# Softmax sums of two head groups folded into the head norm's epsilon, in a two-layer hybrid trunk

## The chip, the cores and the metric

One core of one Trainium2 chip runs the whole program. The metric is the device time of one execution in microseconds (us). Three executions of the kernel before gave 1511.83, 1502.17 and 1504.89 us, a median of 1504.89. The execution that the profiler recorded took 1500.35 us, of which 1498.6 us lie between its first and last instruction (its span).

The engines are TensorE (PE in the profile, with its weight loads as PEld), VectorE (DVE), ScalarE (ACT) and GpSimd (POOL). SyncE (SP) issues most DMAs. Each takes its own instructions strictly in the order in which they were laid down.

## The reference, cut to what matters

Two layers on 512 positions of width 1024. A layer has a mixer of four head groups (A sparse attention, B retention, C gated linear attention, D differential attention), each four heads of 64, and then a squared-ReLU MLP. What the change touches is the end of groups A and D:

```python
def head_norm(y, g, center, dtype):
    ...
    yf = yf * lax.rsqrt(jnp.mean(yf * yf, axis=-1, keepdims=True) + EPS)     # EPS = 1e-6
    yf = yf * g
# group A: one map for each head
    p = jax.nn.softmax(s, axis=-1)
    out = einsum(p, v_sel)
# group D: two maps for each head, a learned lambda
    p = jax.nn.softmax(s, axis=-1)
    w = p[:, :, 0] - lam * p[:, :, 1]
    out = einsum(w, v)
```

A head's output goes straight into `head_norm`. If the softmax is left without its division by the sum m of its row, the output y is m times larger, and the norm gives the same result when eps is replaced by eps times m squared.

## The kernel before, in words

Activations lie as 128 features by 512 positions; weights and activations are split into a high and a low part (`whi`, `wlo`, by ACT and by DVE or POOL), and a projection takes three matmuls for each pair (lines 268 to 270, tiles `ptm`, `ptc`, `po`, `pf`, `p`).

`mixers(l, ...)` (from line 571) emits one layer's mixer. Keys and queries of the indexer come first, then group A's top-k selection on DVE: 48 pairs of MAX8 and MATCH_REPLACE8 (lines 810, 811) for each layer. Then group C in chunks, then D, A and B. The order of D, A and B and of the remaining projections is the token string `PLAN['seq']`: `D00` is head pair 0, block 0 of group D, `8.1` the second row block of projection 8, and so on. Blocks are 128 queries; block b looks at W = 128(b+1) keys.

For a block, `softmax_scores` (line 598) subtracts the row's maximum on DVE (line 602, with the scale and the mask), takes Exp on ACT with the row's sum as a second result (line 604), and takes the sum's reciprocal on DVE (line 608). `d_block` (line 1009) does this for the two maps of each of two heads. It then scales the second map by its reciprocal and by minus lambda (line 1029) and adds the first, scaled by its own (line 1030). `a_block` (line 1042) scales its one map (line 1052), on DVE in six of eight blocks and on ACT in two (`PLAN['xa']`). `pv_block` (line 612) transposes the maps on PE (line 618), copies them out on ACT (line 620) and multiplies by the values (line 623) into one PSUM tile, `yd` or `ya`, of a pool with a single buffer (`yp`). After block 3 `headnorm` (line 580) squares that tile on ACT (`hq`, line 583), sums over the 64 features of each head by a matmul with a block matrix of ones (`hs`, line 585), takes Ln and Exp (lines 587, 588) and multiplies on DVE (line 595), which frees the PSUM tile.

The modulation vectors are matrix-vector products done on DVE (`gemv`, line 277): one DMA of 512 KB into one of two buffers (`gw`) and one reduction of 1024 elements (line 281). In layer 0, 24 of them (three parts of eight columns) are put behind the tokens of projections 8 and 9 and at the output projection. The list `fence` holds an instruction behind which a product emitted later must stand on DVE:

```python
i = gemv(l, part, j, wp.tile([P, DM], F32, name=f"gw{l}_{part}_{j}", tag="graw", bufs=PLAN["gb"]))
for x in fence:
    after(x, i)
```

`fence` is set in three places: at the start of layer 0 to the scaled input `hr` (line 1206), at the end of a pre-norm (line 525), and in `a_block` to the scaling of the last map (line 1054). `after` orders two instructions of the same engine and adds no semaphore.

What is emitted is not yet the order on the engines. A planner walks the program with its own cost estimates and gives each engine, whenever it is free in that estimate, the ready instruction that was emitted first. The resulting order is fixed for the run.

Of the kernel before, what the change touches and what calls it, by code (L numbers as in the profile page):

```python
# [10 lines left out]
F32 = mybir.dt.float32  # L11
# [3 lines left out]
AF = mybir.ActivationFunctionType  # L15
ALU = mybir.AluOpType
# [5 lines left out]
PLAN = {'ah': {},  # L22
 'ap': 'dddd',
 'ar': 'dddd',
 'blo': 'dppd',
 'br': [0, 0, 0, 1],
 'bst': 2,
 'ce': 's',
 'cp': 1,
 'cq': 'a',  # L30
# [59 lines left out]
P = 128  # L90
L = 2
DM = 1024
T = 512
KT = 8
NB = 4
HT = 256
HD = 64
EPS = 1e-6
# [99 lines left out]
def tile_trunk(ctx: ExitStack, tc: tile.TileContext, a, out, dbg=None):  # L198
    nc = tc.nc
    pe, act, dve, pool, sp = nc.tensor, nc.scalar, nc.vector, nc.gpsimd, nc.sync  # L200
# [28 lines left out]
    msk = cp.tile([P, T], F32, name="msk")  # L229
# [8 lines left out]
    eps = cp.tile([P, 1], F32, name="eps")  # L238
    dve.memset(eps, EPS)
    zero = cp.tile([P, 1], F32, name="zero")  # L240
# [5 lines left out]
    nt = ctx.enter_context(tc.tile_pool(name="nt", bufs=2))  # L246
# [28 lines left out]
    fence = []  # L275
# [56 lines left out]
    for i in range(KT):  # L332
        q = nt.tile([P, T], F32, name=f"first_sq{i}", tag="rs" if i % 2 == 0 else "sq", bufs=RS if i % 2 == 0 else 2)
# [8 lines left out]
        e = PLAN["fs"][i // 2:i // 2 + 1]  # L342
# [15 lines left out]
    def rstd(ps, name, n=HT):  # L358
        r = nt.tile([P, n], F32, name="r" + name, tag="nm_r", bufs=1)
        act.activation(r, ps, AF.Ln, bias=eps, scale=1.0 / DM)  # L360
        m = nt.tile([P, n], F32, name="m" + name, tag="rs", bufs=RS)
        dve.tensor_scalar(m, ps, 1.0 / DM, EPS, ALU.mult, ALU.add)
        e = act.activation(r, r, AF.Exp, scale=-0.5)
        t = nt.tile([P, n], F32, name="t" + name, tag="sq")
        dve.tensor_tensor(t, r, r, ALU.mult)
        dve.scalar_tensor_tensor(t, t, -0.5, m, ALU.mult, ALU.mult)
        done[:] = [dve.scalar_tensor_tensor(r, t, 1.5, r, ALU.add, ALU.mult), e]
        return r
# [68 lines left out]
    r1 = rstd(ss1, "first", T)  # L437
# [132 lines left out]
    E = {"p": pool, "d": dve}  # L570

    def mixers(l, h, ch):
# [3 lines left out]
        s0 = st0.enter_context(tc.tile_pool(name=f"s0{l}", bufs=1, side="right", reuse_waits="tile"))  # L576
        stk = ExitStack()
        mx = stk.enter_context(tc.tile_pool(name=f"mx{l}", bufs=1, reuse_waits="tile"))

        def headnorm(i, src):  # L580

            q = nt.tile([P, T], F32, name=f"hq{l}_{i}", tag="sq")
            act.activation(q, src, AF.Square)
            p2 = pj.tile([P, T], F32, name=f"hs{l}_{i}", tag="pj")
            pe.matmul(p2, blk, q, start=True, stop=True)
            r = nt.tile([P, T], F32, name=f"hr{l}_{i}", tag="nm_r", bufs=1)
            act.activation(r, p2, AF.Ln, bias=eps, scale=1.0 / HD)
            act.activation(r, r, AF.Exp, scale=-0.5)
            g = hg[:, l, i:i + 1]
            if 2 <= i < 6:  # L590
                v = nt.tile([P, T], F32, name=f"hv{l}_{i}", tag="rs", bufs=RS)
                dve.tensor_tensor(v, src, r, ALU.mult)
                dve.scalar_tensor_tensor(Y[i], v, g, Y[i], ALU.mult, ALU.mult)
            else:
                dve.scalar_tensor_tensor(Y[i], src, g, r, ALU.mult, ALU.mult)

        NORM = ALU.divide if PLAN['div'] else ALU.mult

        def softmax_scores(ps, mask, W, scale, name):
            s = nt.tile([P, T], F32, name="s" + name, tag="rs", bufs=RS)[:, :W]  # L600
            mn = mx.tile([P, 1], F32, name="mn" + name, tag="mn", bufs=4)
            dve.tensor_tensor_reduce(s, ps, mask, -scale, 3e38, ALU.add, ALU.min, mn)  # L602
            sm = mx.tile([P, 1], F32, name="su" + name, tag="su", bufs=4)
            act.activation(s, s, AF.Exp, bias=mn, scale=-1.0, accum_out=sm)  # L604
            if PLAN["div"]:
                return s, sm
            rc = mx.tile([P, 1], F32, name="rc" + name, tag="rc", bufs=4)
            dve.reciprocal(rc, sm)
            return s, rc

        def pv_block(ps, b, ss, Vs, name):

# [168 lines left out]
        masks = [msk[:, T - P:]]  # L781
        for b in range(1, NB):
            W = P * (b + 1)
# [3 lines left out]
            for hd in range(8):  # L787
                ps = sc.tile([P, T], F32, name=f"ix{l}_{b}_{hd}", tag="sc")[:, :W]
# [4 lines left out]
                e, t = (pool, acp) if hd in PI else (dve, acc)  # L793
# [36 lines left out]
        sums = s1.tile([P, 9, P], F32R, name=f"sums{l}")  # L830
# [71 lines left out]
        for b in range(NB):  # L902
# [3 lines left out]
            for c in range(4):  # L906
# [3 lines left out]
                for hd in range(4):  # L910
                    r = slice(32 * hd, 32 * hd + 32)
                    e = PLAN["qf"][4 * c + hd]
                    f = {"a": act.copy, "p": pool.tensor_copy, "d": dve.tensor_copy}[e]
                    f(Q[r, :, hd, :], QS4[c // 2][r, 2 * (c % 2):2 * (c % 2) + 2, :])  # L914
                ps = sc.tile([P, 2, 4, 64], F32, name=f"sg{l}_{b}_{c}", tag="sc")
# [20 lines left out]
            for hd in range(4):  # L936
                pr, hh = divmod(hd, 2)
# [5 lines left out]
            if b < NB - 1:  # L943
# [6 lines left out]
                s = s1.tile([P, 256], F32, name=f"S{l}_{b}", tag="S", bufs=2)  # L950
                E[PLAN["ms"]].memset(s, 0.0)
                for hd in range(4):
                    r = slice(32 * hd, 32 * hd + 32)
                    c = slice(64 * hd, 64 * hd + 64)
# [46 lines left out]
        def d_open(pr):  # L1001
            QD.append(s1.tile([P, 4, T], F32R, name=f"QD{l}_{pr}", tag="QD", bufs=2))
            KD.append(s1.tile([P, 4, T], F32R, name=f"KD{l}_{pr}", tag="KD", bufs=2))
            for i in range(2):
                d_parts(pr, i)

        def d_block(pr, b):
            if b == 0:
                if pr == len(QD):
                    d_open(pr)  # L1010
            elif b < NB - 1:
                d_parts(pr, b + 1)
            W = P * (b + 1)
            N = max(W, 256)
            sb = []
            for hh in range(2):
                sr = []
                for c in range(2):
                    m = 2 * hh + c
                    ps = sc.tile([P, T], F32, name=f"sd{l}_{pr}_{m}_{b}", tag="sc")  # L1020
                    pe.matmul(ps[:, :N], QD[pr][:, m, b * P:(b + 1) * P], KD[pr][:, m, :N], start=True, stop=True)  # L1021
                    sr.append(softmax_scores(ps[:, :W], msk[:, T - W:], W, 32 ** -0.5, f"D{l}_{pr}_{m}_{b}"))
                (s0, r0), (s1_, r1) = sr
                z = PLAN["xd"][4 * pr + b]
                if z == "a":
                    dve.tensor_tensor(r1, r1, lamv[l], ALU.mult)
                    act.mul(s1_, s1_, r1)
                else:
                    E[z].tensor_scalar(s1_, s1_, r1, lamv[l], ALU.mult, ALU.mult)
                dve.scalar_tensor_tensor(s0, s0, r0, s1_, NORM, ALU.add)  # L1030
                sb.append(s0)
            top(PLAN['top'][4 * pr + b])
            yield
            if b == 0:
                yh[6 + pr] = yp.tile([P, T], F32, name=f"yd{l}_{pr}", tag="yp")
            pv_block(yh[6 + pr], b, sb, [(lambda j, c=64 * (2 * pr + hh): Vd[:, j, c:c + 64]) for hh in range(2)],
                     f"D{l}_{pr}_{b}")
            if b == NB - 1:
                headnorm(6 + pr, yh[6 + pr])

        def a_block(pr, b):
            if b:
                top(max(0, 16 * b + 1 - taken[0]))
            W = P * (b + 1)
            sb = []
            for hh in range(2):
                nme = f"A{l}_{pr}_{hh}_{b}"
                ps = sc.tile([P, T], F32, name="s" + nme, tag="sc")
                two_pass(ps, QS[:, 2 * pr + hh, b * P:(b + 1) * P], 0, max(W, 256))
                s, rc = softmax_scores(ps[:, :W], masks[b], W, HD ** -0.5, nme)  # L1050
                z = PLAN["xa"][4 * pr + b]
                xx = act.mul(s, s, rc) if z == "a" else E[z].tensor_scalar(s, s, rc, None, ALU.mult)
                if PLAN['fence']:
                    fence[:] = [xx]
                sb.append(s)
            yield
            if b == 0:
                yh[pr] = yp.tile([P, T], F32, name=f"ya{l}_{pr}", tag="yp")
            pv_block(yh[pr], b, sb, [lambda j: Va[:, j, :]] * 2, f"A{l}_{pr}_{b}")
            if b == NB - 1:  # L1060
                headnorm(pr, yh[pr])

        def b_rope(b):
            if b == 0:
# [33 lines left out]
        QD, KD, QB, yh = [], [], [], {}  # L1098
# [8 lines left out]
        for tok in PLAN["seq"].split():  # L1107
            k = tok[0]
# [16 lines left out]
            else:  # L1125
                g, b = tok.split(".")
# [9 lines left out]
    ident = cp.tile([P, P], F32, name="ident")  # L1136
    blk = cp.tile([P, P], F32, name="blk")
# [3 lines left out]
    lamv = [cp.tile([P, 1], F32, name=f"nlam{l}") for l in range(L)]  # L1141
# [228 lines left out]
    h, ch = h_tiles("h10_"), None  # L1370
    for l in range(L):
        h, ch = rest(l, mixers(l, h, ch))
# [26 lines left out]
```

## Time and profile before

| | |
|---|---|
| median of three executions | 1504.89 us (1502.17 to 1511.83) |
| profiled execution | 1500.35 us, span 1498.6 us |
| mean granted TensorE clock | 0.981 |
| PE busy | 1424.6 us, 95% of the span |
| weight loads busy | 1190.9 us, 79% |
| DVE busy | 990.7 us, 66% |
| ACT busy | 742.3 us, 50% |
| POOL busy | 280.5 us, 19% |

Busy shares are means over stages with different limits. The mixers are at about 50 to 330 us (layer 0) and 800 to 1066 us (layer 1) of the span; the rest is output projection and MLP.

### The profile page before, as it was taken

The page shows a single profiled execution, that of the slowest core. Times are in us where ns is not written, and L with a number is a line of the kernel's source. Part 1 is how long each engine was busy: PE and PEld are TensorE (multiplying, and loading weights), DVE is VectorE, ACT ScalarE, POOL GpSimd, SP SyncE. Part 2 cuts the span into 40 slices and gives each one's busy share as a digit, 9 for nine tenths or more (in the row PEclk, how much of TensorE's full clock was granted, in tenths as well). Part 3 has the DMA queues.
Part 4 walks back from the last instruction along what each step waited for, and adds up shares of the span by engine and source line. Part 5 has one row for each costly group of instructions (what it writes and reads, how often), then busy time and mean ns, then how long its engine had stood idle before and what let it go on. Part 6 is the DMA issues. An engine that isn't in the chain of part 4 may idle for free.

```text
span 1498.6 us, 23592 instructions
## 1 busy us (share of the span) xinstructions
PE 1424.6 (95%) x8514; PEld 1190.9 (79%) x8514; DVE 990.7 (66%) x2209; ACT 742.3 (50%) x1655; POOL 280.5 (19%) x268
## 2 busy tenths in 40 slices
PE   7989999999999999999989899999999999999996
PEld 4667878768898878888978769787789888888896
DVE  8798878786796875434477999753678334343435
ACT  4667486656453323324257575855765333242322
POOL 3244321335100000000032443213430000000001
PEclk8999999999999999999999999999999999999999
DMA  9420223466078884333131102211531433333301
GB/s 340 140 68 14 78 71 99 150 205 222 29 245 288 294 268 155 92 99 92 43 113 59 57 15 72 71 43 56 163 104 52 126 93 94 97 97 93 94 20 57
DMA packets 82269, 171.12 MB, mean 114 GB/s; under 512 B 9284, under 2 KB 16102, under 8 KB 81896
## 3 DMA queue, kind: packets, MB, share of 16 engines
q1 hardware_dynamic: 79524, 167.47, 35.7%
q10 hardware_dynamic: 2628, 2.14, 0.4%
q8 instruction: 67, 1.10, 0.3%
q14 instruction: 50, 0.41, 0.1%
HBM read 165.39 MB, written 4.19 MB: 113 GB/s over the span
## 4 chain that ended last, share of the span: by engine, by line
PE 71%; DVE 17%; ACT 4%; DMA 4%; issue 2%; POOL 1%; SPq 0%; DVEq 0%; ACTq 0%; POOLq 0%
PE p L269 7%; PE p L270 7%; PE p L268 7%; PE pf L269 7%; PE pf L270 7%; PE pf L268 7%; PE ptm L268 3%; PE ptm L269 3%; PE ptm L270 3%; DVE ia L797 2%; DVE m L810 2%; DVE ia L811 2%; PE first L1186 1%; DMA gw<-modw 1%; PE firstk L1186 1%
## 5 line engine op out<-in xcount | busy, mean ns | idle before, releaser
L262 ACT CAST whi<-raw 128x512 fp32r<-128x512 f32 x388 | 237.3, 621 | 355.9 <-PE p L269 157.9
L264 DVE TENSOR_TENSOR wlo<-raw,whi 128x512 fp32r<-128x512 f32 x266 | 190.8, 722 | 205.7 <-ACT whi L262 194.1
L264 POOL TENSOR_TENSOR wlo<-raw,whi 128x512 fp32r<-128x512 f32 x122 | 165.1, 1371 | 330.0 <-ACT whi L262 279.7
L461 POOL TENSOR_TENSOR sapost<-sapost,sqpost 128x256 f32<-128x256 f32 x16 | 12.3, 771 | 671.6 <-ACT sqpost L459 671.6
L281 DVE CUSTOM_DVE_ANT_0 gw<-gw,cond 128x1024 f32<-128x1024 f32 x80 | 101.3, 1269 | 40.6 <-DMA gw<-modw 40.2
L810 DVE MAX8 m<-ia 128x8 f32<-128x256 f32 (+2 forms) x96 | 53.1, 556 | 1.3
L811 DVE MATCH_REPLACE8 ia<-m,ia 128x256 f32<-128x256 f32 (+2 forms) x96 | 52.0, 542 | 0.0
L914 ACT COPY QF<-q 32x256 f32<-32x256 f32 x120 | 48.4, 403 | 5.5 <-DVE q L891 2.5
L1288 DVE TENSOR_TENSOR rf<-rf,pf 128x512 f32<-128x512 f32 (+1 forms) x80 | 45.8, 574 | 2.6 <-ACT rf L1287 2.5
L1287 ACT ACTIVATE rf<-pf 128x512 f32<-128x512 f32 (+1 forms) x80 | 40.5, 507 | 5.6 <-PE pf L270 5.6
L923 PE MATMUL sg<-QF,KF 128*64 128x256 f32 x224 | 30.5, 395 | 11.0 <-DVE AC L929 8.2
L602 DVE CUSTOM_DVE_ANT_0 sD<-sd,msk 128x128 f32<-128x128 f32 (+3 forms) x64 | 29.6, 488 | 16.8 <-PE sd L1021 12.0
L604 ACT ACTIVATE sD<-sD,mnD 128x128 f32<-128x128 f32 (+3 forms) x64 | 35.5, 559 | 6.8 <-DVE mnD L602 6.4
L890 POOL TENSOR_TENSOR KF<-F,kc 128x512 f32<-128x512 f32 x16 | 23.9, 1502 | 43.7 <-ACT F L883 42.4
L268 PE MATMUL p<-hd_7h,whi 128*128 128x512 f32 (+1 forms) x80 | 28.6, 358 | 3.1 <-ACT hd_7h L471 3.1
L923 PEld LDWEIGHTS sg<-QF,KF 128*64 128x64 f32 x224 | 14.6, 137 | 21.0 <-issue 13.7
L269 PE MATMUL pf<-h_5l,whi 128*128 128x512 f32 (+1 forms) x80 | 28.0, 350 | 2.8 <-DVE h_5l L515 2.8
L797 DVE SCALAR_TENSOR_TENSOR ia<-rl,wi,ia 128x256 f32<-128x256 f32 (+2 forms) x42 | 29.0, 708 | 2.2 <-ACT rl L791 1.0
L269 PE MATMUL p<-hd_7l,whi 128*128 128x512 f32 (+1 forms) x80 | 28.3, 353 | 0.6 <-DVE hd_7l L472 0.6
L268 PE MATMUL ptm<-whi,h_0h 128*128 128x256 f32 x74 | 25.4, 345 | 3.5 <-ACT h_0h L511 3.5
L467 PE MATMUL sspre<-sapre,ones 128*128 128x256 f32 x48 | 17.3, 474 | 12.0 <-POOL sapre L461 7.1
L268 PE MATMUL p<-hd_0h,whi 128*128 128x512 f32 (+1 forms) x80 | 28.4, 355 | 0.0
(623 smaller groups left out, 5002.2 us busy)
## 6 DMA issues: line engine op xcount, KB each, us to landing
raw<-w SPq DMA_DIRECT2D x256, 256.0 KB, 2.7
gw<-modw SPq DMA_DIRECT2D x80, 512.0 KB, 4.2
raw<-wtm SPq DMA_DIRECT2D x76, 256.0 KB, 2.8
gs<-modw SPq DMA_DIRECT2D x16, 512.0 KB, 6.3
raw<-wo SPq DMA_DIRECT2D x32, 256.0 KB, 2.7
raw<-wtc SPq DMA_DIRECT2D x24, 256.0 KB, 2.8
xin<-xT SPq DMA_DIRECT2D x8, 256.0 KB, 3.5
wq<-wtm SPq DMA_DIRECT2D x8, 256.0 KB, 6.4
```

Source lines behind the costliest of these rows:

```text
L262: act.copy(hi, raw)
L264: (lo_eng or dve).tensor_tensor(lo, raw, bits(hi), ALU.subtract)
L268: pe.matmul(ps, l[0], r[0], start=start, stop=False)
L269: pe.matmul(ps, l[0], r[1], start=False, stop=False)
L270: pe.matmul(ps, l[1], r[0], start=False, stop=stop)
L281: return dve.tensor_tensor_reduce(raw, raw, cond, 1.0, 0.0, ALU.mult, ALU.add, modT[l][:, c:c + 1])
L797: e.scalar_tensor_tensor(t, rl, wi[:, b, hd:hd + 1], t, ALU.mult, ALU.add)
L810: dve.max(m8, acc)
L811: dve.match_replace(acc, m8, acc, MARK)
L914: f(Q[r, :, hd, :], QS4[c // 2][r, 2 * (c % 2):2 * (c % 2) + 2, :])
L923: pe.matmul(ps[t, i], KF[:, lv, t], Q[:, i, :, t], start=True, stop=True)
L1288: dve.tensor_tensor(rl, rl, ps, ALU.mult)
```

## The change

The reciprocals of A's sums, the scaling of A's maps and the setting of `fence` in `a_block` go. The sums of A's map and of D's first map are kept in a tile of 128 by 4 blocks by 2 heads for each head pair. In D the second map is multiplied by minus lambda times m0/m1 and added to the unscaled first map: a reciprocal and one operation on 128 by 1, then one operation on the maps. `headnorm` of the four head pairs of A and D gets the sums: it squares them, scaled by the root of 64 eps and spread over 64 columns (`he`, one ACT operation on 128 by 512), and adds them to the block sum by four matmuls with the identity as moving operand; Ln is then taken with a bias of zero.

```diff
-        def headnorm(i, src):
+        def headnorm(i, src, sums=None):
             q = nt.tile([P, T], F32, name=f"hq{l}_{i}", tag="sq")
             act.activation(q, src, AF.Square)
             p2 = pj.tile([P, T], F32, name=f"hs{l}_{i}", tag="pj")
-            pe.matmul(p2, blk, q, start=True, stop=True)
+            pe.matmul(p2, blk, q, start=True, stop=sums is None)
+            if sums is not None:
+                e = nt.tile([P, NB, 2, HD], F32, name=f"he{l}_{i}", tag="sq")
+                act.activation(e, sums.unsqueeze(3).broadcast_to([P, NB, 2, HD]), AF.Square, scale=(HD * EPS) ** 0.5)
+                for b in range(NB):
+                    pe.matmul(p2[:, P * b:P * b + P], e[:, b].rearrange("p h d -> p (h d)"), ident, start=False, stop=b == NB - 1)
             r = nt.tile([P, T], F32, name=f"hr{l}_{i}", tag="nm_r", bufs=1)
-            act.activation(r, p2, AF.Ln, bias=eps, scale=1.0 / HD)
+            act.activation(r, p2, AF.Ln, bias=eps if sums is None else zero, scale=1.0 / HD)
...
-        def softmax_scores(ps, mask, W, scale, name):
+        def softmax_scores(ps, mask, W, scale, name, sm):
...
-            sm = mx.tile([P, 1], F32, name="su" + name, tag="su", bufs=4)
             act.activation(s, s, AF.Exp, bias=mn, scale=-1.0, accum_out=sm)
-            if PLAN["div"]:
-                return s, sm
-            rc = mx.tile([P, 1], F32, name="rc" + name, tag="rc", bufs=4)
-            dve.reciprocal(rc, sm)
-            return s, rc
+            return s
+
+        heads_sum = {}
+
+        def sum_of(k, pr, b, hh):
+            if (k, pr) not in heads_sum:
+                heads_sum[k, pr] = mx.tile([P, NB, 2], F32, name=f"hsum{l}_{k}{pr}", tag="hsum", bufs=4)
+            return heads_sum[k, pr][:, b, hh:hh + 1]
...
-                (s0, r0), (s1_, r1) = sr
...
-                    E[z].tensor_scalar(s1_, s1_, r1, lamv[l], ALU.mult, ALU.mult)
-                dve.scalar_tensor_tensor(s0, s0, r0, s1_, NORM, ALU.add)
+                (s0, m0), (s1_, m1) = sr
+                rt = mx.tile([P, 1], F32, name=f"rt{l}_{pr}_{hh}_{b}", tag="rc", bufs=4)
+                dve.reciprocal(rt, m1)
+                dve.scalar_tensor_tensor(rt, rt, m0, lamv[l], ALU.mult, ALU.mult)
+                dve.scalar_tensor_tensor(s0, s1_, rt, s0, ALU.mult, ALU.add)
...
-                s, rc = softmax_scores(ps[:, :W], masks[b], W, HD ** -0.5, nme)
-                z = PLAN["xa"][4 * pr + b]
-                xx = act.mul(s, s, rc) if z == "a" else E[z].tensor_scalar(s, s, rc, None, ALU.mult)
-                if PLAN['fence']:
-                    fence[:] = [xx]
-                sb.append(s)
+                sb.append(softmax_scores(ps[:, :W], masks[b], W, HD ** -0.5, nme, sum_of("A", pr, b, hh)))
```

## Rows read from the trace of the kernel before

**Rows 1.** The page: busy us, share of the span, instructions; then the chain's shares.
```profile
PE 1424.6 (95%) x8514; PEld 1190.9 (79%) x8514; DVE 990.7 (66%) x2209; ACT 742.3 (50%) x1655; POOL 280.5 (19%) x268
...
PE 71%; DVE 17%; ACT 4%; DMA 4%; issue 2%; POOL 1%; SPq 0%; DVEq 0%; ACTq 0%; POOLq 0%
```
**Rows 2.** Windows by stage; columns in the first line.
```profile
core 0: us, PE busy (x) PEld busy (x) DVE busy (x) ACT busy (x) POOL busy (x), PEclk, DMA share, GB/s
50.00:182.00 132.00, 119.27 (x792) 95.07 (x791) 118.18 (x310) 87.26 (x220) 58.34 (x57) 0.97 0.21 61
182.00:330.00 148.00, 143.77 (x936) 111.57 (x937) 113.08 (x308) 95.80 (x240) 39.91 (x31) 0.97 0.38 124
922.00:1066.00 144.00, 139.57 (x942) 108.82 (x941) 88.35 (x270) 97.21 (x244) 40.41 (x34) 1.00 0.20 59
```
**Rows 3.** Groups by line, DVE: busy us, mean ns of one, idle before.
```profile
L1030 DVE SCALAR_TENSOR_TENSOR sD<-sD,rcD,sD 128x128 f32<-128x128 f32 (+3 forms) x32 | 20.4, 638 | 0.4
L1029 DVE TENSOR_SCALAR sD<-sD,rcD,nlam 128x128 f32<-128x128 f32 (+3 forms) x32 | 14.7, 459 | 0.9
L1052 DVE TENSOR_SCALAR sA<-sA,rcA 128x128 f32<-128x128 f32 (+3 forms) x24 | 10.9, 455 | 0.5
L608 DVE RECIPROCAL rcD<-suD 128x1 f32<-128x1 f32 x64 | 9.9, 159 | 8.3 <-ACT sD L604 7.6
```
**Rows 4.** Groups by line, ACT: A's scaling, and the head norm's Square.
```profile
L1052 ACT ACTIVATE sA<-sA,rcA 128x256 f32<-128x256 f32 (+1 forms) x8 | 4.2, 555 | 0.2 <-DVE rcA L608 0.2
...
L583 ACT ACTIVATE hq<-yd 128x512 f32<-128x512 f32 x4 | 2.4, 599 | 0.8 <-PE yd L623 0.7
```
**Rows 5.** Timeline of PE at 86 and at 247 us: start, us, instruction.
```profile
86.36 1.15 PE L842 MATMUL z<-wa,caT 17*128 17x128 f32 x8
87.45 0.50 PE L268 MATMUL ptc_t<-h_5h,whi 128*128 128x512 f32 x1
...
247.45 1.02 PE L585 MATMUL hs<-hq,blk 128*128 128x512 f32 x2
247.91 0.68 PE L268 MATMUL ptm<-whi,h_0h 128*128 128x256 f32 x1
```
**Rows 6.** Waits of PE, 182 to 332 us: waiter, releaser, us in total, times, longest.
```profile
PE sd L1021 <- DVE mnD L602: 4.6, 2, 3.6
```
**Rows 7.** The same of layer 1, 915 to 1075 us.
```profile
PE sd L1021 <- DVE mnD L602: 2.1, 2, 1.0
```
**Rows 8.** Timelines of SP and DVE: the products' first DMA, and where products stand.
```profile
42.10 0.33 SPq L279 DMA_DIRECT2D gw<-modw  x1
...
286.97 0.97 DVE L1052 TENSOR_SCALAR sA<-sA,rcA 128x512 f32<-128x512 f32 x1
287.87 2.29 DVE L281 CUSTOM_DVE_ANT_0 gw<-gw,cond 128x1024 f32<-128x1024 f32 x1
...
416.35 0.48 DVE L515 SCALAR_TENSOR_TENSOR h_7l<-vpre,modT,h_7h 128x256 fp32r<-128x256 f32 x1
...
417.76 1.22 DVE L281 CUSTOM_DVE_ANT_0 gw<-gw,cond 128x1024 f32<-128x1024 f32 x1
```
**Rows 9.** The page's group of the products: busy us, mean ns, idle before.
```profile
L281 DVE CUSTOM_DVE_ANT_0 gw<-gw,cond 128x1024 f32<-128x1024 f32 x80 | 101.3, 1269 | 40.6 <-DMA gw<-modw 40.2
```
**Rows 10.** Timelines of DVE and PE: first D softmax, first output projection, both layers.
```profile
181.38 0.28 DVE L602 CUSTOM_DVE_ANT_0 sD<-sd,msk 128x128 f32<-128x128 f32 x1
...
329.62 0.39 PE L268 MATMUL po<-yT_0h,whi 128*128 128x256 f32 x1
...
922.19 0.29 DVE L602 CUSTOM_DVE_ANT_0 sD<-sd,msk 128x128 f32<-128x128 f32 x1
...
1065.56 0.39 PE L268 MATMUL po<-yT_0h,whi 128*128 128x256 f32 x1
```
**Rows 11.** Busy DVE of the top-k's MAX8 (line 810), 50 to 182 us.
```profile
50.00:182.00 132.00, 26.54 (x48) 0.97 0.21 61
```

More of the change, by code (lines that the diff above doesn't have):

```diff
@@ L595, in headnorm @@
                 dve.scalar_tensor_tensor(Y[i], src, g, r, ALU.mult, ALU.mult)
-        NORM = ALU.divide if PLAN['div'] else ALU.mult
-        def softmax_scores(ps, mask, W, scale, name):
+        def softmax_scores(ps, mask, W, scale, name, sm):
             s = nt.tile([P, T], F32, name="s" + name, tag="rs", bufs=RS)[:, :W]
@@ L1021, in d_block @@
                     pe.matmul(ps[:, :N], QD[pr][:, m, b * P:(b + 1) * P], KD[pr][:, m, :N], start=True, stop=True)
-                    sr.append(softmax_scores(ps[:, :W], msk[:, T - W:], W, 32 ** -0.5, f"D{l}_{pr}_{m}_{b}"))
-                (s0, r0), (s1_, r1) = sr
[L1024 to L1028, printed above, removed]
-                    E[z].tensor_scalar(s1_, s1_, r1, lamv[l], ALU.mult, ALU.mult)
-                dve.scalar_tensor_tensor(s0, s0, r0, s1_, NORM, ALU.add)
+                    sm = mx.tile([P, 1], F32, name=f"su{l}_{pr}_{m}_{b}", tag="su", bufs=4) if c else sum_of("D", pr, b, hh)
+                    sr.append((softmax_scores(ps[:, :W], msk[:, T - W:], W, 32 ** -0.5, f"D{l}_{pr}_{m}_{b}", sm), sm))
+                (s0, m0), (s1_, m1) = sr
[3 more added lines that the diff above has]
+                dve.scalar_tensor_tensor(s0, s1_, rt, s0, ALU.mult, ALU.add)
                 sb.append(s0)
@@ L1038, in d_block @@
             if b == NB - 1:
-                headnorm(6 + pr, yh[6 + pr])
+                headnorm(6 + pr, yh[6 + pr], heads_sum["D", pr])
         def a_block(pr, b):
@@ L1060, in a_block @@
             if b == NB - 1:
-                headnorm(pr, yh[pr])
+                headnorm(pr, yh[pr], heads_sum["A", pr])
         def b_rope(b):
```

## The prediction

> **What bounds the kernel now.** I read the page first: PE is busy for 95% of the span and carries 71% of the chain that ended last, DVE carries 17% [rows 1]. The reader should see there that taking work from DVE pays only where DVE makes PE wait. So I read the windows next, for the stretches in which the softmaxes lie. From the first D softmax to the output projection PE is busy 143.77 of 148 us in layer 0 and 139.57 of 144 in layer 1 [rows 2]: 4.2 and 4.4 us of idle PE, and no more than these 8.6 us can be won there by shortening any other engine's chain. The stretch ahead of it in layer 0 is another matter: from 50 to 182 us DVE is busy 118.18 of 132 us, with 13.8 us idle, and PE 119.27, with 12.7 us idle [rows 2]. There DVE sets much of the pace. The waits come third: of PE's idle time the softmax chain accounts for little. PE waits 4.6 us for the row maxima in layer 0, of which 3.6 are one wait at the very start of D, behind the end of top-k, so 1.0 is left; in layer 1 it is 2.1 us [rows 6, 7].
>
> **DVE work removed.** For each layer D has 16 heads times blocks. Each loses one scaling of 459 ns and one reciprocal of 159 ns, and gains one operation on 128 by 1. No row shows that operation with two per-row operands; it lies between a reciprocal (159 ns) and the mean of the wide operation (638 ns), and being 128 by 1 I take 159 [rows 3]. So D loses 16 x 0.459 = 7.3 us for each layer, and the wide operation that stays keeps its 638 ns. A loses 16 reciprocals (2.5 us) and 12 scalings of 455 ns (5.5 us) on DVE, and 4 of 555 ns (2.2 us) on ACT [rows 3, 4]. That is 15.3 us of DVE a layer, 30.6 in all, 2% of the span as a sum of busy time. Almost all of it lies beside a full PE. What comes off the path is bounded by the PE waits above, 1.0 + 2.1 us; I take **-2**, since both waits have Exp and the maximum in their chain too, and these stay. The lower end is 0. The upper end is all idle PE of both stretches, 8.6 us.
>
> **PE work added.** The head norm of two pairs of D and two of A in two layers makes 8 calls, with four full-precision matmuls each, 128 weight columns and 128 moving columns. The nearest row is the gate matmul `z`: also four of 128 weight columns by 128 moving columns, recorded as 8 instructions. It starts at 86.36 and the next matmul of the stream starts at 87.45, so the four take 1.09 us; its contraction is over 17 rows instead of 128, and I take the time to be the same [rows 5]. The lower bound is 0.46 us, the step from the start of `hs` at 247.45 to the next matmul, 512 columns with one set of weights [rows 5], and none at all where PE would have idled. The upper bound is double 1.09. I take 1.09, the same shapes: 8 x 1.09 = **+8.7**; the ends are 0 and 17. There is no cover: at 247.45 `hs` is followed by a projection's matmul without a gap [rows 5], so whatever is put between them moves the rest of the layer.
>
> **ACT work added.** One Square of 128 by 512 in each call, 599 ns as `hq` [rows 4], 4.8 us in all, against 4.4 us of A's scalings that go [rows 4]: nothing. It depends on the sums only, so it can run ahead of `hq`; if it stands behind, it runs under the `hs` matmul. **New waits.** PE's four matmuls wait for that Square, and the Ln for them. The PSUM tile of the pair is free about 1.1 us later, and the next pair's value products wait for it; PE has projections to do meanwhile, so I cost it at nothing, and at 1.1 us for each of 8 calls if these run out. The Square's result also takes the second of two `sq` buffers, which the rotary operations of A and B use: a rotary operation behind a head norm starts about 1 us later on DVE, and the softmax queued behind it too. Both have room under PE.
>
> **The fence that goes.** This is the part that the diff says least about. In layer 0 the 24 modulation products stand on DVE behind A's scalings: the one at 287.87 follows the scaling of 286.97 directly [rows 8]. With that scaling gone, the list still holds the instruction of line 1206, done before 50 us. The trace shows what the planner does with a free product: the DMA of the first was issued at 42.10, and after the pre-norm's last instruction at 416.35 the products start at 417.76, ahead of where they were emitted [rows 8]. So I expect most of them to move from 246-345 us to the stretch that begins at 50 us. Two prices follow. Where they leave, the end of layer 0 gets lighter: from the first D softmax to the output projection layer 0 takes 148.2 us and layer 1, with no products there, 143.4 [rows 10]. The bound on the gain is 4.9 us; I take **-3**. Where they arrive, 24 x 1.27 = 30.5 us [rows 9] meet 13.8 us of idle DVE. The excess of 16.7 us pushes something: top-k, which has 48 MAX8 of 26.5 us together [rows 11] and as many replacements, is emitted after the C chunks and needed only by A, so it can slip into the D stretch, where the removed scalings make room. C's and D's own operations are delayed only while a product already runs. I take **+3** for PE; the ends are 0 and 16.7 plus the DMA waits, 0.50 us for each product as before (40.2/80 [rows 9]), 12 us, together 28.7. SP's queue counts too: a product's DMA waits there for one of two buffers, and the weight DMAs stand behind it.
>
> **The sum**: -2 + 8.7 - 3 + 3 = +6.7 us, made against the profiled execution's 1500.35 us: 1507. The median of the runs shown is 4.5 us above that execution, so against it I forecast 1504.89 + 6.7, about **1511 us**.
>
> **Weighed against the skill.** The rows give PE 95% as matmul time and 79% as weight loads [rows 1]. The Trainium skill, "Trainium Kernel Development and Optimization", section "Best Practices", says that matmul busy time is a poor measure of distance from the limit, and to go by the share of weight loads. By that PE would have a fifth to spare, the four matmuls would find room and the sum would be -2. That is the second rival; against it stands the stream without gaps at 247 us [rows 5].
>
> **Rivals.** (1) *Slower: the products block DVE early.* Place: 50 to 182 us of layer 0 on DVE. Price: the excess of 16.7 us, up to 28.7 with DMA waits, on top of 8.7 - 2 - 3 = +3.7; about 1525 us, up to 1537. It decides once the products take more than the idle DVE there and top-k cannot slip freely. For it: DVE is 90% busy there [rows 2], and a product that has started holds everything else for 1.27 us. Against: D's stretch has 35 us of idle DVE [rows 2]. (2) *PE has room.* The added matmuls fall into PE's gaps, and the rest is -2 - 3 + 3: 1503 us. (3) *Faster: the idle PE vanishes.* The lighter DVE closes the 8.6 us of idle PE and the full 4.9 us are won, with the added matmuls half hidden (+4.4) and the products absorbed: -9.1, 1496 us. For it: the shorter chain of D; against: the waits that name the softmax are 3.1 us, not 8.6 [rows 6, 7]. (4) *The fence changes nothing*, because buffers or the queue hold the products where they are: -2 + 8.7 = +6.7, the forecast's own number; it is counted there.
>
> **How the numbers follow.** Forecast (with 4) 0.50, rival 1 0.22, rival 2 0.18, rival 3 0.10. About 1% is what a measurement of this kernel can tell from no change: 15 us, so 1490 and 1520. Slower by more: nearly all of rival 1 and a little of the forecast, 0.22. Faster by more: the far half of rival 3, 0.05. Within: 0.73. The forecast's own range is 1503 to 1518; with rivals 2 and 3 and the middle of rival 1, the range for 8 in 10 is 1496 to 1529.
>
> **What would show it.** PE: `hs` with four more matmuls in eight calls, about 1.09 us each, and PE busy up by some 9 us. DVE busy down by some 30 us. Products on DVE from about 50 us, top-k ending later than 181 us, the stretch from the first D softmax to the output projection about 3 us shorter than its 148.2 plus 4 x 1.09 in layer 0, and about 3 us longer in layer 1. Wrong if layer 1 gets shorter (then the softmax chain was the limit), or if PE's idle time in 50 to 182 us grows by over 10 us (rival 1).

## The result and the profile after

Four executions of the kernel after have a median of 1517.39 us, four of the kernel before, on the same chip, 1504.04. The ratio over all executions is 1.0075, interval [1.0051, 1.0100]: 11.3 us slower (the medians are 13.4 apart), where +6.7 was forecast. The median lies just inside the upper end of the forecast's range of 1503 to 1518 us. A second comparison, among the experiments, gave 1.0067 [1.0047, 1.0087]. The profiled execution took 1513.37 us, with a span of 1511.6.

First the page of the kernel after: busy times, shares of the chain, and the groups that answer to [rows 1, 3, 9].

```profile
PE 1428.8 (95%) x8578; PEld 1193.8 (79%) x8578; DVE 967.9 (64%) x2121; ACT 743.5 (49%) x1655; POOL 281.8 (19%) x268
...
PE 64%; DVE 21%; DMA 7%; issue 4%; ACT 3%; POOL 0%; SPq 0%; ACTq 0%; DVEq 0%; POOLq 0%
...
L281 DVE CUSTOM_DVE_ANT_0 gw<-gw,cond 128x1024 f32<-128x1024 f32 x80 | 101.1, 1264 | 27.6 <-DMA gw<-modw 27.3
...
L1035 DVE SCALAR_TENSOR_TENSOR sD<-sD,rt,sD 128x128 f32<-128x128 f32 (+3 forms) x32 | 19.2, 600 | 0.7
...
L1034 DVE SCALAR_TENSOR_TENSOR rt<-rt,hsum_D,nlam 128x1 f32<-128x1 f32 x32 | 7.4, 230 | 0.6
```

PE has the same share of busy time as before, 95%, with 4.2 us more (7.7 in a second profile of the same kernel, where some 9 was forecast). DVE is busy for 22.8 us less, yet the kernel is slower: here the work taken from DVE shows in its busy time and not in the span. The new 128 by 1 operation takes 230 ns, not 159. DVE's wait for the products' DMAs fell from 40.2 to 27.3 us, a first sign that the products moved.

The next view cuts the span where [rows 10] cut that of before: the first D softmax and the first output projection of each layer (columns: start and end, length, then busy us of PE, PEld, DVE, ACT, POOL, granted clock of PE, DMA share, GB/s). Kernel after:

```profile
50.00:188.83 138.83, 119.51 (x796) 94.52 (x794) 132.41 (x314) 87.17 (x219) 65.33 (x57) 0.98 0.43 143
188.83:340.34 151.51, 144.63 (x957) 112.28 (x957) 91.92 (x271) 96.14 (x240) 36.39 (x31) 0.98 0.18 57
...
928.44:1076.59 148.15, 142.92 (x970) 111.80 (x968) 78.14 (x225) 97.01 (x242) 39.70 (x34) 1.00 0.20 58
```

The same stretch of the kernel before, up to its first D softmax:

```profile
50.00:181.40 131.40, 118.99 (x791) 94.79 (x789) 117.58 (x306) 86.96 (x219) 58.34 (x57) 0.97 0.20 60
```

It grew from 131.4 us to 138.8. DVE is busy 132.4 us of it, 95%, while PE has the same work as before and idles 19.3 us instead of 12.4. In layer 1 no product stands in these stretches, and it grew as well, from 143.4 to 148.1 us. Two timelines show what stands there now: first PE at the first head norm of layer 0, then DVE at the start of D (columns: start, us, instruction).

```profile
230.16 1.12 PE L586 MATMUL hs<-hq,blk 128*128 128x512 f32 x2 [0.46 <-ACT hq L584]
231.13 1.05 PE L591 MATMUL hs<-ident,he 128*128 128x128 f32 x8
231.94 0.36 PE L268 MATMUL ptm<-whi,h_0h 128*128 128x256 f32 x1
```

```profile
50.93 2.32 DVE L281 CUSTOM_DVE_ANT_0 gw<-gw,cond 128x1024 f32<-128x1024 f32 x1
...
186.69 0.67 DVE L818 MATCH_REPLACE8 ia<-m,ia 128x512 f32<-128x512 f32 x1
187.29 1.61 DVE L281 CUSTOM_DVE_ANT_0 gw<-gw,cond 128x1024 f32<-128x1024 f32 x1
188.83 0.08 DVE L281 DVE_READ_ACCUMULATOR2_ANT modT<- 128x1 f32 x1
188.83 0.28 DVE L607 CUSTOM_DVE_ANT_0 sD<-sd,msk 128x128 f32<-128x128 f32 x1
...
206.31 0.69 DVE L817 MAX8 m<-ia 128x8 f32<-128x512 f32 x1
```

The four added matmuls (eight instructions) stand between `hs` and a projection's matmul. The first product stands at 50.93 us and the last directly ahead of the first D softmax; top-k still runs at 206 us, inside D (in the kernel before its last operation of the layer starts at 179.69 us). PE's wait for that softmax grew from the 3.6 us of [rows 6] (waits of PE, 50 to 190 us: total, times, longest):

```profile
PE sd L1028 <- DVE mnD L607: 5.4, 1, 5.4
```

### The profile page after: what moved, and what is told of

It is laid out like the page before. It is cut to its first block, busy times and chain, and to the rows that moved or that the text cites. A ratio compares the mean times of both kernels' runs of the same rounds, so it can differ in the third digit from the quotient of the medians.

```text
span 1511.6 us, 23609 instructions
## 1 busy us (share of the span) xinstructions
PE 1428.8 (95%) x8578; PEld 1193.8 (79%) x8578; DVE 967.9 (64%) x2121; ACT 743.5 (49%) x1655; POOL 281.8 (19%) x268
## 4 chain that ended last, share of the span: by engine, by line
PE 64%; DVE 21%; DMA 7%; issue 4%; ACT 3%; POOL 0%; SPq 0%; ACTq 0%; DVEq 0%; POOLq 0%
PE p L269 6%; PE p L268 6%; PE p L270 6%; PE pf L269 6%; PE pf L270 6%; PE pf L268 6%; DMA gw<-modw 5%; PE ptm L268 3%; PE ptm L269 3%; PE ptm L270 3%; DVE gw L281 2%; DVE ia L818 2%; DVE m L817 2%; PE po L269 1%; PE po L270 1%
## 5 line engine op out<-in xcount | busy, mean ns | idle before, releaser
L461 POOL TENSOR_TENSOR sapost<-sapost,sqpost 128x256 f32<-128x256 f32 x16 | 12.3, 770 | 669.1 <-ACT sqpost L459 668.9
L281 DVE CUSTOM_DVE_ANT_0 gw<-gw,cond 128x1024 f32<-128x1024 f32 x80 | 101.1, 1264 | 27.6 <-DMA gw<-modw 27.3
L1287 ACT ACTIVATE rf<-pf 128x512 f32<-128x512 f32 (+1 forms) x80 | 40.5, 507 | 5.9 <-PE pf L270 5.8
L607 DVE CUSTOM_DVE_ANT_0 sA<-sA,ia 128x256 f32<-128x256 f32 (+2 forms) x24 | 12.9, 556 | 28.6 <-PE sA L786 27.1
L930 PEld LDWEIGHTS sg<-QF,KF 128*64 128x64 f32 x224 | 14.5, 137 | 19.3 <-issue 11.4
L1081 DVE TENSOR_TENSOR pb<-sb,gam 128x512 f32<-128x512 f32 (+3 forms) x32 | 14.8, 481 | 21.7 <-PE yr L1088 18.4
L269 PE MATMUL p<-hd_0l,whi 128*128 128x512 f32 (+1 forms) x80 | 28.3, 354 | 0.0
```

The source lines that it names most:

```text
L269: pe.matmul(ps, l[0], r[1], start=False, stop=False)
L281: return dve.tensor_tensor_reduce(raw, raw, cond, 1.0, 0.0, ALU.mult, ALU.add, modT[l][:, c:c + 1])
L930: pe.matmul(ps[t, i], KF[:, lv, t], Q[:, i, :, t], start=True, stop=True)
```

## The experiments

Two theories stood against each other. **M**: the added matmuls are the cost, because PE's stream is full. **F**: the cost is the fence that went, since the products then fill DVE early. Each kernel has 4 to 12 executions, compared with those of the kernel before on the same chip. Stage lengths come from one profile each. In microseconds, "to D" is the start of the first D softmax of layer 0, and L0 and L1 run from a layer's first D softmax to its output projection:

| kernel | ratio, interval | to D | L0 | po to next D | L1 |
|---|---|---|---|---|---|
| before | 1 | 181.4 | 148.2 | 592.6 | 143.4 |
| after | 1.0075 [1.0051, 1.0100] | 188.8 | 151.5 | 588.1 | 148.1 |
| after, again | 1.0067 [1.0047, 1.0087] | 190.0 | 151.6 | 591.0 | 149.6 |
| after, fence at A | 1.0063 [1.0043, 1.0084] | 181.5 | 155.1 | 595.7 | 148.2 |
| before, no fence at A | 1.0019 [1.0004, 1.0033] | 188.1 | 151.1 | 593.0 | 144.5 |
| after, no eps term | 1.0038 [1.0020, 1.0055] | 189.8 | 149.5 | 593.5 | 144.7 |
| after, fence at A, no eps term | 1.0012 [0.9998, 1.0025] | 181.6 | 154.5 | 596.2 | 144.6 |
| after, matmuls in fp32r | 1.0025 [1.0009, 1.0041] | 188.8 | 149.0 | 587.5 | 146.4 |
| same, fence at D | 1.0038 [1.0018, 1.0058] | 184.9 | 160.1 | 588.2 | 146.4 |
| same, fence at top-k | 1.0023 [1.0009, 1.0038] | 183.2 | 156.1 | 587.4 | 146.4 |
| before, fence at D | 0.9987 [0.9970, 1.0004] | 182.2 | 153.9 | 587.2 | 144.6 |
| before, 4 matmuls added | 1.0066 [1.0043, 1.0088] | 181.6 | 155.5 | 587.0 | 146.9 |
| before, 8 matmuls added | 1.0067 [1.0044, 1.0090] | 182.0 | 156.8 | 591.2 | 151.7 |
| before, ten products early | 0.9987 [0.9975, 0.9999] | 184.3 | 150.8 | 589.4 | 144.5 |

The kernel after stands there twice. The same program's stages differ by up to 2.9 us between two profiles, so a smaller difference of one profile against one other says nothing; what follows is read from values that repeat over several kernels. The row of the kernel before is one profile too, of a short execution: 1500.35 us, where its medians beside the experiments are 1506.6 to 1507.5.

Part of this scatter is the clock of PE. In layer 1 the two profiles of the kernel after have the same wait of PE for `pb`, 0.7 us. In the first the granted clock is 1.00 over the whole stretch; in the second it falls to 0.83 near the stretch's end, and L1 is 149.6 instead of 148.1 us (window of the second):

```profile
1070.00:1080.00 10.00, 9.26 (x27) 3.20 (x28) 7.72 (x9) 5.07 (x9) 4.80 (x4) 0.83 0.34 106
```

**1. The fence put back** (M against F), behind the maximum of A's last map:

```diff
+                last_max[:] = [dve.tensor_tensor_reduce(s, ps, mask, -scale, 3e38, ALU.add, ALU.min, mn)]
...
+                fence[:] = last_max[:]
```

> The changed kernel with one thing put back: the modulation products of layer 0 again stand on DVE behind group A's softmax (behind the maximum of its last map, since the scaling is gone). Theory M (the loss is the matmuls added to PE: 8 calls x 1.09 us, seen as +4.8 us in layer 1 between the first D softmax and the output projection, where no product runs): still slower than before by 8 to 10 us, ratio 1.005 to 1.007. Theory F (the loss is the products in the DVE-bound stretch, where the first D softmax came 7.4 us later): nearly back to before, ratio 1.000 to 1.002.

1.0063: M. "To D" returns to 181.5, but the time does not. L0 is 155.1 us with the fence and 151.5 and 151.6 without: here layer 0 gets shorter behind the start of D when the products leave it.

**2. The fence alone taken out of the kernel before**, by deleting `fence[:] = [xx]`:

> The kernel before with one thing taken away: group A's scaling no longer holds back the modulation products; every division is still there. Theory M: what the products lose early (about 7 us) they give back behind the first output projection (the trace of the changed kernel shows 4.5 us there), ratio 1.000 to 1.002. Theory F: ratio 1.005 to 1.008, as the change.

1.0019: M again, +2.9 us. The start of D moves by 6.7 us, much as in the kernel after. M's place for the return, behind the output projection, is not shown: the stretch there is 593.0 against 592.6 us, and no stage of this profile is shorter than in the kernel before. The two profiled executions are 12.3 us apart, since the one of the kernel before was a short one. Why only 2.9 of the 6.7 us are left stays open.

**3. No eps term**: the Square of the sums and the four matmuls go, with a plain eps in Ln, so eps is not scaled by the squared sums.

```diff
-                e = nt.tile([P, NB, 2, HD], F32, name=f"he{l}_{i}", tag="sq")
...
+            act.activation(r, p2, AF.Ln, bias=eps, scale=1.0 / HD)
```

> The changed kernel without the Square of the sums and the four matmuls in the head norm: plain eps is added, so the small term eps times the squared sum is left out. Theory M: 9 us faster than the changed kernel, ratio to before 0.999 to 1.002. Theory F: as the changed kernel, 1.006 to 1.008.

1.0038 lies between the two: neither theory alone. L1 falls to 144.7.

**4. Both**: the fence back and no eps term; what is left of the change is the lighter DVE (the same part is left out).

> Both at once: products behind group A's maxima as before, and no Square of the sums and no four matmuls (the term eps times the squared sum is left out). What is left of the change is only the DVE and ACT work removed. If that work lay beside a full PE, as forecast: 0 to 3 us faster than before, ratio 0.998 to 1.000. If the softmax chain was the limit: up to 8.6 us faster, ratio 0.994 to 0.996.

1.0012, where 0.998 to 1.000 had been expected: the removed division gives nothing that can be measured. The view of waits of layer 1 tells why (PE, 925 to 1082 us):

```profile
PE sd L1024 <- DVE mnD L602: 2.3, 3, 0.9
PE thA L659 <- DVE hlA L655: 1.1, 2, 0.9
PE sb L1075 <- DVE pb L1078: 0.7, 1, 0.7
```

The kernel before has 2.1 us of waits for the maxima there [rows 7], the kernel before without its fence 3.2:

```profile
PE sd L1021 <- DVE mnD L602: 3.2, 2, 2.2
```

Here PE waits 2.3 us for the maxima and, in DVE's new order, 1.1 us for `hlA`: 3.4 together, no less than in either. DVE's busy time in that stretch fell by 10 us (88.69 us in the kernel before without its fence, 78.19 here), and the stretch kept its length (144.55 and 144.61). Taking the fence out costs more in this pair: 1.0012 with it, 1.0038 without (experiment 3), while L0 is 154.5 us with it and 149.5 without.

```profile
932.25:1076.80 144.55, 138.96 (x937) 108.20 (x935) 88.69 (x269) 96.85 (x242) 40.05 (x34) 1.00 0.20 59
```

```profile
932.40:1077.01 144.61, 139.35 (x938) 108.12 (x936) 78.19 (x225) 95.26 (x238) 39.66 (x34) 1.00 0.20 59
```

**5. The matmuls in one pass.** `he` and the identity are held as fp32r:

```diff
-                e = nt.tile([P, NB, 2, HD], F32, name=f"he{l}_{i}", tag="sq")
+                e = nt.tile([P, NB, 2, HD], F32R, name=f"he{l}_{i}", tag="sq")
...
-                    pe.matmul(p2[:, P * b:P * b + P], e[:, b].rearrange("p h d -> p (h d)"), ident, start=False, stop=b == NB - 1)
+                    pe.matmul(p2[:, P * b:P * b + P], e[:, b].rearrange("p h d -> p (h d)"), identr, start=False, stop=b == NB - 1)
```

> The kernel after, with the squared sums and the identity of the head norm's four matmuls in the rounded fp32r type (one pass each instead of two); the eps term is rounded to that type. Theory M (the added matmuls stand in PE's full stream and cost what they last): the four matmuls of a call last some 0.45 us instead of 0.88, so 8 calls give back 3 to 4 us: ratio to the kernel before 1.0045 to 1.0060, and the layer-1 stretch from the first D softmax to the output projection 146 to 147 us, between the 148.1 with them and the 144.7 without. Theory W (the cost is not the columns but the wait for the Square of the sums and the changed order): no gain, 1.0065 to 1.0085, stretch 148 us.

L1 is 146.4 in all three kernels with fp32r, 1.8 us above the 144.6 without the matmuls: 0.45 us a call, as M has it, against W. The ratio of 1.0025 is lower than M's 1.0045; against the second comparison of the kernel after it is 0.42% less, with intervals of 0.16 and 0.20% either way. That is 6.3 us where M had 3 to 4; part of it goes with the granted clock (see experiments 9 and 10).

**6, 7, 8. The products elsewhere.** The fence is set by D's last map operation or by the last one of the top-k, on the fp32r kernel; then by D's on the kernel before, in place of A's.

```diff
-                dve.scalar_tensor_tensor(s0, s1_, rt, s0, ALU.mult, ALU.add)
+                fence[:] = [dve.scalar_tensor_tensor(s0, s1_, rt, s0, ALU.mult, ALU.add)]
```

> As the run with fp32r identity matmuls, and the fence is set to the last operation on a D block's maps, so that the products stand behind D's softmaxes and ahead of A's. Theory F (the products in 50 to 189 us cost what they add to that stage, 7 us, and most of that stays to the end): first D softmax back at 181 to 182 us and a ratio of 0.999 to 1.001. Theory S (the products cost about the same wherever they stand, since their transfers hold DVE wherever they meet it; earlier ones free what follows): D starts at 181.5 but the stretch to the output projection is 154 us or longer and the ratio is 1.003 to 1.006, that of the kernel with fp32r alone.

> As the run with fp32r identity matmuls, and the fence is set to the last operation of the top-k, so that the products stand in D's stretch behind the top-k (from about 182 us). Theory F: the first D softmax at 181 to 182 us, ratio 0.999 to 1.001, since D's stretch has over 35 us of idle DVE. Theory S: a product that runs holds a softmax chain for 1.3 us each, 24 of them in D's stretch; the stretch to the output projection is over 152 us and the ratio 1.003 to 1.006.

> The kernel before (divisions kept), with the fence set to the last operation on a D block's maps in place of A's scaling. Theory F (where the products stand matters by itself): they leave the last 40 us of layer 0 and do not reach the stretch before D; ratio 0.997 to 0.999, and the stretch from the first D softmax to the output projection under 148 us. Theory S: no change, 0.9995 to 1.0015.

F missed its ratios on the fp32r kernel (1.0038 and 1.0023 against 0.999 to 1.001). S is nearer there, though 1.0023 is below its 1.003: the start of D improves by 4 to 6 us, and L0 gives it back, 160.1 and 156.1 us. On the kernel before, 0.9987 is in F's span but cannot be told from 1, and L0 is 153.9 us where F had under 148. The waits of DVE show what L0 pays (182 us to the output projection; the first line is of the kernel before, the second of the kernel before with the fence at D):

```profile
DVE gw L281 <- DMA gw<-modw: 5.5, 6, 2.5
```

```profile
DVE gw L281 <- DMA gw<-modw: 13.5, 9, 4.9
```

Behind D the 24 products stand closer together, from 241 to 315 us instead of 247 to 350, and DVE waits longer for their transfers. In the same kernel PE's wait for `sapre` at the output projection, 3.4 us with the fence at A, is 1.5, but a wait for `h_5l` appears that the kernel before does not have (waits of PE, 60 us from the first output projection; before, then fence at D).

```profile
PE sspre L467 <- DVE sapre L461: 3.4, 1, 3.4
```

```profile
PE sspre L467 <- DVE sapre L461: 1.5, 1, 1.5
PE pf L269 <- DVE h_5l L515: 1.4, 1, 1.4
```

PE's busy time in these 60 us is 55.83 and 56.27: 0.4 us gained, not 1.9. The kernel after has the same two waits, of 1.5 and 1.4 us.

**9, 10. The cost alone, on the kernel before.** Four, then eight matmuls a call, of a Square scaled by zero:

```diff
+            more = 4 if i in (0, 1, 6, 7) else 0
+            pe.matmul(p2, blk, q, start=True, stop=not more)
+                act.activation(e, eps.broadcast_to([P, T]), AF.Square, scale=0.0)
+                    pe.matmul(p2[:, c], e[:, c], ident, start=False, stop=k == more - 1)
```

> The kernel before, divisions and fence kept, with four fp32 matmuls against the identity and a Square of 128 by 512 added in each of the eight head norms of A and D, as in the kernel after, but of a constant scaled by zero, so that nothing is computed with them. Theory M (the matmuls cost their length, 0.88 us a call): 7 us in all, ratio 1.004 to 1.006, the layer-1 stretch from the first D softmax to the output projection 3.5 us longer than its 143.4 to 144.6. Theory W (with the divisions kept, DVE sets the pace beside PE and covers a part): 1.000 to 1.003.

> As the run with four added matmuls on the kernel before, with eight in each call. Theory M: twice the cost, ratio 1.008 to 1.012 and the layer-1 stretch 7 us longer than before's. Theory W (a fixed cost of the call, the Square or the wait for it): the same as with four.

Four give 1.0066 with divisions and fence untouched, above W's span and above M's 1.004 to 1.006, which its interval takes in: a cost of the size of the whole change's. Eight give 1.0067, and M's 1.008 is missed. In layer 1 the dose counts, between kernels in which PE's waits for the maxima are the same: four give 146.9 against 143.4 us (2.1 us of such waits in both), eight 151.7 against the 144.5 to 144.6 of the other kernels with the division (3.2 us). Laid against the kernel before, each call of four moves every later matmul by 0.88 to 0.90 us. The two timelines of PE at one call (four, then eight matmuls):

```profile
249.78 1.02 PE L586 MATMUL hs<-hq,blk 128*128 128x512 f32 x2
250.64 1.05 PE L592 MATMUL hs<-ident,he 128*128 128x128 f32 x8
251.45 0.36 PE L268 MATMUL ptm<-whi,h_0h 128*128 128x256 f32 x1
```

```profile
251.04 1.02 PE L586 MATMUL hs<-hq,blk 128*128 128x512 f32 x2
251.90 1.95 PE L592 MATMUL hs<-ident,he 128*128 128x128 f32 x16
253.60 0.36 PE L268 MATMUL ptm<-whi,h_0h 128*128 128x256 f32 x1
```

The step from the matmuls to the projection behind them is 0.81 us with four and 1.70 with eight; a fixed cost of the call (W) would not double. The whole kernel does not show the second four: each interval reaches 0.23% either way, and the difference sought, 7 us, is 0.46%.

The clock of PE hides part of it. Each execution's mean granted clock is on record, and in every kernel the longer executions tend to be those with the lower clock: with four matmuls they run from 1505.80 us at 0.982 to 1523.04 at 0.974. A line fitted through the executions of all kernels gives 1.05 us for each 0.001. The mean clock is 0.978 with four and 0.981 with eight. Set to 0.980 by that line (an estimate; no run held the clock), the kernel before comes to 1506.4 to 1506.5 us on each of the three chips, and above it lie four matmuls by 7.8 us, eight by 12.0, the kernel after by 10.3, fp32r by 7.0, the kernel before without its fence by 6.4 and the next experiment's by 1.2. So the second four would cost 4.2 us, each of these figures having a standard error of some 0.7, and fp32r would give back 3.4, as M had it. The clock can itself be an effect of the edit, so this is a hint and not a measurement.

**11. Ten products early**, the rest behind A:

```diff
-                for x in fence:
+                for x in fence0 if l == 0 and (part == 2 or part == 3 and j < 2) else fence:
```

> The kernel before, divisions kept; of layer 0's 24 products the first ten are let go from the fence of A's scaling and keep only the one at the start of the layer, the other fourteen stay behind A. Ten products are 12.7 us of DVE against the 13.8 us that it idles there between 50 and 182 us. Theory F (the cost is what exceeds DVE's idle time): the first D softmax at 182 to 184 us, and layer 0's end and output projection 3 to 4 us shorter, ratio 0.996 to 0.999. Theory S (each product costs about the same wherever it stands): 0.9995 to 1.002.

0.9987 [0.9975, 0.9999]: the ratio is F's, the start of D, 184.3 us, is just beyond F's, and what was gained (589.4 against 592.6 us behind the output projection) is no more than two profiles of one program differ by. It is the only one here whose interval lies below 1, and just so: one of a dozen kernels, with a mean clock of 0.982 where the kernel before has 0.980. A gain is not shown by that. It is faster than the kernel after, and that owes nothing to the folded division.

**12. The kernel after, again**:

> The kernel after unchanged, beside the others on one chip: with the first comparison's 1.0075 it is 1.005 to 1.008. The sum of what the single edits gave (eps matmuls 0.37 to 0.51%, the fence 0.12 to 0.26%, the divisions that go 0.0 to 0.1%) puts it at 1.005 to 1.008 as well; below 1.004 the fp32r run has no gain that is shown.

1.0067: the size stands, and it lies in the 1.005 to 1.008 that the single edits add up to.

## Why the prediction was right, step by step

- **The sign and the mechanism held**: the time stayed within 1% on the slow side, and the added matmuls carry most of it. The sum of +6.7 us is short of the 10.1 to 11.3 us measured (1.0067 and 1.0075), by three terms.
- **DVE work removed, -2**: no gain is shown, which was the end given. The division's removal with everything else undone gave 1.0012 [0.9998, 1.0025], and without the matmuls L1 is 144.6 and 144.7 us without the divisions, 143.4 to 144.6 with them. The 1.0 and 2.1 us of waits [rows 6, 7] were not shortened: the order changed with the work, and a wait for `hlA` appeared. Busy DVE fell by 22.8 us, not 30; the new 128 by 1 operation at 230 instead of 159 ns is 2.3 us of that.
- **PE work added, +8.7**: L1 rose by 3.5 us (148.1 and 148.2 against 144.6 and 144.7; on the kernel before 146.9 against 143.4) for four calls, 0.88 us each instead of the 1.09 of `z`. That is 7.0 in all if layer 0 costs the same; its stretches, with the products in them, differ by 0.6 to 7.3 us and cannot tell. Over whole executions the matmuls cost 0.29 to 0.51% (after, again, against no eps term; fence at A with and without it), 4.4 to 7.7 us, and 9.9 us on the kernel before. "No cover" held in every layer-1 profile. That PE has room (second rival) is refuted there: every layer-1 stretch with added matmuls (146.4 to 151.7 us) is longer than every one without (143.4 to 144.7), by their length where the other waits are equal. The Trainium skill ("Trainium Kernel Development and Optimization", "Best Practices") judges the distance from the limit by MFU, the arithmetic done as a share of the peak, together with the share of weight loads. The forecast took the weight loads alone, and as room for more matmuls: in layer 1, where the weight loads fill 108.82 of 144 us [rows 2], there was none.
- **ACT and the new waits, nothing**: held as far as can be seen. The Square `he` took 620 ns, and over the 32 instructions of `hs` PE waited for `hq` once, for 0.5 us.
- **The fence, -3 and +3**: the products went where they were expected, but D began 7.4 us later, not 3: the price of their arrival was put at less than half. The gain where they left is seen on the kernels with the folded division (L0 155.1 us with the fence, 151.5 and 151.6 without; without the eps term 154.5 and 149.5), though a part of it may be the clock (0.97 against 0.98 in these stretches, 0.95 against 0.96). It does not show on the kernel before (148.2 and 151.1), whose 148.2 us is the one short profile. What its removal costs over whole executions is 2.9 us on the kernel before (1.0019), 3.9 on the kernel after without the eps term, and 0.6 to 1.8 on the kernel after: some 3 us, known to no better than that.
- **The sum as measured**: 0 + 7.0 + 2.9 = 9.9 us. It is near the whole, but its terms are of two kinds: 7.0 is a step of PE's stream times eight, the others are differences of whole executions, whose intervals reach some 2 us either way.
- **Luck**: -2 and +8.7 come to 6.7, where 0 and 7.0 come to 7.0. Two errors offset each other, and what is missing in the forecast is the fence.
- **Products that block DVE early (first rival)**: its place and mechanism are there (19.3 us of idle PE up to D, 12.4 before), at less than half its price of 16.7. Top-k slipped into D, as the forecast's argument had it; whether that kept the price down was not tested. **Faster** found no support: no kernel with the folded division is faster than the one before.

## What to carry to other kernels

Ask first which engine's stream is full in the stage that is touched. Here work moved from an engine with gaps to the full one cost its whole length in layer 1, and 32 matmuls of 0.22 us each outweighed 28 us of DVE operations (groups of 40.5 us that go, 12.5 that come). And read what a removed instruction held up: here it was the fence of 24 unrelated operations, the first of which moved from 246.75 us to 50.93. They delayed one place by 7.4 us, and some 3 us of it were left at the end. Before a stage of two profiles is compared, one of the kernels should be profiled twice, and the clock granted in the stage and in the executions belongs beside the lengths.

## What the runs showed of the hardware

A fall of PE's clock can follow a short wait, and then costs beside it. In the kernel with the fence at A and no eps term, PE waits 2.76 us for `pb` at the end of layer 0. First its timeline, then the windows of that place:

```profile
321.68 1.12 PE L1085 MATMUL yr<-pb,Vb 128*64 128x256 f32 x2 [2.76 <-DVE pb L1078]
```

```profile
318.00:320.00 2.00, 0.65 (x2) 0.19 (x2) 2.00 (x3) 1.31 (x3) 2.00 (x2) 1.00 0.73 227
320.00:322.00 2.00, 0.32 (x1) 0.29 (x2) 2.00 (x6) 0.00 (x0) 0.57 (x2) 0.71 0.79 244
322.00:324.00 2.00, 2.00 (x6) 0.51 (x4) 2.00 (x3) 0.00 (x0) 2.00 (x2) 0.50 0.07 29
...
328.00:330.00 2.00, 2.00 (x4) 0.67 (x2) 2.00 (x5) 0.73 (x2) 0.00 (x0) 0.50 0.80 214
330.00:332.00 2.00, 2.00 (x7) 0.69 (x6) 1.73 (x4) 1.18 (x3) 0.00 (x0) 0.73 0.75 234
```

PE is busy 0.97 of 4 us. In the second half of that the granted clock falls to 0.71, and from 322 to 330 us it is 0.50, the lower level of 1.2 GHz, although PE is busy throughout; in the next slice it is 0.73. At half the clock for some 9 us, a PE that is never idle loses about 4.5 us, more than the wait (an estimate from these rows). It does not follow each time: in the kernel with eight matmuls PE waits 2.19 us for `pb` at the same place and does nothing in this slice, and the clock stays at 1.00 there and up to 346 us:

```profile
324.00:326.00 2.00, 0.00 (x0) 0.00 (x0) 2.00 (x7) 1.05 (x3) 0.00 (x0) 1.00 0.35 90
```

It may be one reason why stages of layer 0 answer to a change of DVE's order by more than the wait that is seen; that was not tested.

Two prices were also off: the 128 by 1 operation with two per-row operands took 230 ns where a reciprocal of that shape takes 159 [rows 3], and a full-precision matmul of 128 by 128, recorded as two instructions, moved the stream by 0.22 us (0.89 for four), in fp32r as one instruction by 0.11 (1.8 us of layer 1 for sixteen).
